# Neighbourhood attention: key planes loaded in pieces over several ticks, memory scores held eight ticks apart

## The chip, the cores and the metric

The kernel runs on one core of one Trainium2 chip. The metric is device time in microseconds (us) of one execution. Three runs of the kernel before give a median of 2871.68 us, with 2870.42 and 2873.8 as the lowest and the highest.

## What is computed

The layer mixes 2048 tokens of 1024 channels (a grid of 32 rows by 64 columns) in three ways in parallel, merges the three branches by gates, adds the result to the input, and ends with an MLP. Two of the branches matter here: attention over a window of 8 rows by 16 columns around each token (8 heads of 32 channels), and attention into 256 memory tokens (4 heads of 64 channels).

```python
def hybrid_layer(...):
    h = rmsnorm(x, g_mix)
    z = h @ w_in
    qk_m, v_m, o_m, i_pre, f_pre, qkv_na, q_mem, gate_pre = jnp.split(z, split_idx, axis=-1)
    ...                                     # mLSTM branch -> h_m
    q_na = rmsnorm(q_na, g_na_q) * (NA_HEAD_DIM ** -0.5)
    k_na = rmsnorm(k_na, g_na_k)
    h_na = neighbourhood_attention(q_na, k_na, v_na, rpb)
    h_mem = memory_cross_attention(q_mem, rmsnorm(mem, g_mem), w_mem_kv, g_mem_q, g_mem_k)
    gates = jax.nn.sigmoid(gate_pre).reshape(bsz, s, N_BRANCH, D_MODEL)
    y = (gates[:, :, 0] * (h_m @ w_proj_mlstm) + gates[:, :, 1] * (h_na @ w_proj_na)
         + gates[:, :, 2] * (h_mem @ w_proj_mem))
    x = x + y @ w_out
    u = rmsnorm(x, g_ffn) @ w_up
    return x + jnp.square(jax.nn.relu(u)) @ w_down
```

All of it is float32.

## The kernel before, in words

**Products.** A float32 operand is split into a high plane and a low plane, and a product is three matmuls: high by high, high by low, low by high (`mm3`, lines 243 to 245). A weight unit of 512 KB is loaded into one of three raw buffers (`wr`, line 183), split by ScalarE (line 186) and VectorE (line 187) into one of five `ws` buffers, and then multiplied.

**Phases.** Phase 1 goes over four blocks of 512 tokens (`block_a`): query and key projections of the window attention, convolution channels, values, mLSTM values, gate channels (blocks 2 and 3 only), output gates. Phase 2 runs the mLSTM chunks beside the other gate channels, phase 3 the merge, the output projection and the MLP. The window attention and the memory attention belong to phase 1: the first score of the window attention stands at 109.7 us of the profile and the last at 891.9 us.

**Ticks.** Within the projections of phase 1, the program stops after every six matmuls or so (`tick`), and each stream may put some instructions of its own there: `unit_stream` for the preparation of queries and keys, another one for the memory attention (`mem_unit`), and `na_stream` for the window attention. TensorE's order is written out by hand in this way. The other engines and the DMA queue are ordered by a scheduler at build time, which goes by priorities. Nearly all DMAs are issued by SyncE (SP), in one in-order queue; a DMA that has to wait for a buffer holds up those behind it.

**Window attention.** Its work comes in groups `g` of four grid rows and head halves `hg` of four heads: 16 pairs of (g, hg). A pair has one tile of queries, `naq` (96 partitions), and one of keys, `nak` (96 partitions, 4 heads, up to 704 columns). The 96 partitions hold 32 channels three times, so that one matmul (line 1084) makes the three products at once: queries as high, high, low and keys as high, low, high. `na_load_qk` fills both tiles from the scratch tensors `s_qs` and `s_ks` with six DMAs, each on 32 partitions and all four heads, issued in the tick in which the unit is made. Each pair is used by two units (column halves) of four heads, and each head has one score matmul (`na_scores`), one bias tile `nab` (line 1075, four buffers), a fused add and maximum on VectorE (line 1088), an exponential on ScalarE (line 1090), transposes (line 1104) and values (line 1118). Heads come every four ticks in blocks 0 to 2 (`na_rate` 1) and every two ticks in block 3 (`na_rate` 2).

**Memory attention.** `mem_unit` makes one unit for each 128 tokens: normalise, transpose, then twelve score matmuls (line 1314) into two score banks, a maximum on VectorE, four exponentials (line 1321) on ScalarE, transposes (line 1334) whose results ScalarE copies out (line 1336), and values (line 1344). Two units are live at once and both move in ticks with `tk` 3, thus every four ticks; `mem_at` only keeps two units from scoring in the same tick. The scores of the window and of the memory attention, and their values, share three PSUM banks (`mx`).

**Other traffic of phase 1 on the same queue.** The results of a gate group are stored from one of two `ev` buffers (`s_g`), and sums of the down weights are made beside them: `xt` loads (line 440) and `s_t` stores.

Of the kernel before, what the change touches and what calls it, by code (L numbers as in the profile page):

```python
# [13 lines left out]
F32 = mybir.dt.float32  # L14
# [16 lines left out]
EV = {1: 2, 2: 2, 3: 8}  # L31
XT = 2
PREP_V = 2
RMS_0, MEM_LOAD = 2, 2
NA_LATER, NA_VALUES = 5, 3
NAB = 4
LATER_3 = 4
# [45 lines left out]
class Body:  # L83
    def __init__(self, tc, a):
        self.tc, self.nc, self.a = tc, tc.nc, a
        self.n = 0
        self.later, self.ahead = LATER, AHEAD
        self.streams, self.qkq, self.memq, self.aux_end = [], [], [], False
        self.na_ready, self.na_end, self.na_rate, self.tk = [], False, 1, 0
        self.na_v, self.na_vfree, self.scored = [], 2, False  # L90
        self.ticks, self.mem_at = 0, -1
        self.jobs, self.out, self.split = [], (), ()
        self.wplan, self.wready = self.plan(), []

# [879 lines left out]
    def na_stream(self):  # L974


        todo, fetched, prev, ready = [], [], [], []
        biases, freed = [], [0] * NAB
        cur = last = None
        late = False  # L980
        while True:
            while self.na_ready:
                g = self.na_ready.pop(0)
                todo += [(g, hg, half) for hg in range(2) for half in range(2)]
            if todo and not fetched and (cur is None or cur["h"] > 0):
                last = self.na_unit(*todo.pop(0), last, 4 if cur else 8)
                fetched.append(last)
                biases += [(last, h) for h in range(4)]
            if cur is None and not fetched and self.na_end and not prev and not ready:
                return  # L990
            if self.tk % 2:
                due = ready.pop(0)[1] if ready and ready[0][0] >= NA_VALUES and not self.scored else None
                if due and (self.na_rate == 2 or late):
                    self.na_values(due)
                    due, late = None, False
                late = bool(ready and ready[0][0] >= NA_VALUES)
                self.scored = False
                step = self.tk == 3 or self.na_rate == 2
                if step and prev and prev[0][0] >= NA_LATER:
                    u, h, sb = prev.pop(0)[1]  # L1000
                    self.na_transpose(u, h, sb)
                    if h == 3:
                        ready.append([0, u])
                if due:
                    self.na_values(due)
                if step:
                    if cur is None and fetched and fetched[0]["wait"] <= 0:
                        cur = fetched.pop(0)
                    if cur:
                        while len(cur["bias"]) <= cur["h"]:  # L1010
                            self.na_bias(*biases.pop(0))
                            freed.pop(0)
                        freed.append(3)
                        prev.append([0, self.na_scores(cur, cur["h"])])
                        cur["h"] += 1
                        if cur["h"] == 4:
                            cur = None
            for u in fetched:
                u["wait"] -= 1
            for x in prev + ready:  # L1020
                x[0] += 1

            freed = [max(n - 1, 0) for n in freed]
            if biases and freed and not freed[0]:
                self.na_bias(*biases.pop(0))
                freed.pop(0)
            yield

    def na_load_qk(self, g, hg, kr0, nr):
        nc = self.nc  # L1030
        q = self.p_a.tile([96, 4, 256], F32R, name=f"naq{g}_{hg}", tag="naq", bufs=2)
        k = self.p_a.tile([96, 4, 11 * 64], F32R, name=f"nak{g}_{hg}", tag="nak", bufs=2)
        qs = self.scr["qs"][:, g, hg].rearrange("(h d) l f t -> d h l (f t)", d=32)
        ks = self.scr["ks"][:, hg, :, kr0 * 64:(kr0 + nr) * 64].rearrange("(h d) l t -> d h l t", d=32)

        for i, (lq, lk) in enumerate(((0, 0), (0, 1), (1, 0))):
            ds = slice(32 * i, 32 * i + 32)
            nc.sync.dma_start(q[ds].bitcast(F32), qs[:, :, lq])
            nc.sync.dma_start(k[ds, :, :nr * 64].bitcast(F32), ks[:, :, lk])
        return q, k  # L1040

    def na_unit(self, g, hg, half, before, wait):

        nc = self.nc
        kr0 = min(max(4 * g - 4, 0), 24)
        nr = 8 if g in (0, 7) else 11
        u = dict(g=g, hg=hg, half=half, nk=nr * 40, pts=[], h=0, wait=wait)
        u["qk"] = before["qk"] if half else self.na_load_qk(g, hg, kr0, nr)
        u["kts"] = [(3 * i, min(3, nr - 3 * i)) for i in range((nr + 2) // 3)]
        u["ho"] = before["ho"] if half else self.t("nho", [128, 2, 256], 1, F32R)  # L1050
        u["bias"] = []
        self.na_v.append(u)
        self.na_load_v()
        return u
# [242 lines left out]
    def mem_unit(self, b, t, z):  # L1297
        nc = self.nc
        yield from self.mem_norm(z)
        yield  # L1300
        q = self.t("mq", [128, 2, 2, 128], 2, F32R)
        self.mem_trans(z, q, self.gmqk[:, 0:1])
        yield

        while self.mem_at == self.ticks:
            yield
        es = []
        self.scored, self.mem_at = True, self.ticks
        psc = [self.ps("mx", (128, 2, 256)) for _ in range(2)]
        for p in range(2):  # L1310
            for i, (lq, lk) in enumerate(((0, 0), (0, 1), (1, 0))):
                for j in range(2):
                    js = slice(j * 64, j * 64 + 64)
                    nc.tensor.matmul(psc[j][:, p], q[js, lq, p], self.mk[js, lk, p], start=i == 0, stop=i == 2)
        nms, sms = ([self.small(2, "m") for _ in range(2)] for _ in range(2))
        for nm, pj in zip(nms, psc):
            nc.vector.tensor_reduce(nm, pj, AX.X, ALU.max, negate=True)
        for nm, sm, pj in zip(nms, sms, psc):
            e = self.t("me", [128, 2, 256], 4)
            for p in range(2):  # L1320
                nc.scalar.activation(e[:, p], pj[:, p], AF.Exp, bias=nm[:, p:p + 1], accum_out=sm[:, p:p + 1])
            es.append(e)
        for e, sm in zip(es, sms):
            rs = self.small(2, "m")
            nc.vector.reciprocal(rs, sm)
            nc.vector.tensor_tensor(e, e, rs.unsqueeze(2).to_broadcast([128, 2, 256]), ALU.mult)
        yield
        yield
        ptp = []
        for e in es:  # L1330
            tp = self.ps("tr", (128, 4, 128))
            for p in range(2):
                for kt in range(2):
                    nc.tensor.transpose(tp[:, 2 * p + kt], e[:, p, kt * 128:(kt + 1) * 128], self.ident)  # L1334
            pT = self.t("mpT", [128, 4, 128], 4)
            nc.scalar.activation(pT, tp, AF.Copy)
            ptp.append(pT)
            yield
        po = self.ps("mx", (128, 4, 128))
        for p in range(2):  # L1340
            for kt in range(2):
                for j in range(2):
                    h = 2 * p + j
                    nc.tensor.matmul(po[j * 64:(j + 1) * 64, p], self.mv[:, kt, h * 64:(h + 1) * 64], ptp[j][:, 2 * p + kt],  # L1344
                                     start=kt == 0, stop=kt == 1, tile_position=(0, j * 64))
        ho = self.t("mho", [128, 2, 2, 128], 1, F32R)
        nc.scalar.activation(ho[:, 0], po[:, 0:2], AF.Copy)
        nc.vector.tensor_tensor(ho[:, 1], po[:, 0:2], ho[:, 0].bitcast(F32), ALU.subtract)
        t0 = b * TB + t * 128
        self.store(self.scr["hmem"][:, :, :, t0:t0 + 128], ho.bitcast(F32))  # L1350
# [377 lines left out]
```

## Time and profile before

| | |
|---|---|
| median of the runs | 2871.68 us |
| the profiled execution, its own time | 2871.6 us |
| its span, from the first to the last instruction | 2869.9 us |
| TensorE busy | 2844.7 us |
| DMA, share of the 16 engines' span on the main queue | 67.1% |
| key loads (`nak`) | 36 of 352 KB and 12 of 256 KB |
| query loads (`naq`) | 48 of 128 KB |

In the lines of the trace, L12 is line 12 of the kernel. PE is TensorE (PEld its weight loads), DVE VectorE, ACT ScalarE, POOL GpSimd, SP SyncE. "Idle before" is the time that an engine waited ahead of an instruction, with the releaser that came last. "DMA share" is the mean busy share of the 16 DMA engines, GB/s what they moved. A line of the chain of waits has its start, its length and what it is.

### The profile page before, as it was taken

To read this page: it belongs to the slowest core of one execution; us is meant where nothing else is said; L and a number is where in the kernel's file an instruction comes from. 1 tells how busy PE (TensorE), PEld (TensorE's weight loads), DVE (VectorE), ACT (ScalarE), POOL (GpSimd) and SP (SyncE) were. 2 spreads that over 40 slices of the span, in tenths; PEclk is the share of its full clock that TensorE was granted. 3 is DMA by queue.
4 is the path that set the end of the run, shared out by engine and by line. 5 is a ranking of instruction groups with operands and counts; after the bars stand their busy time and mean duration, and the time that the engine had idled before them with its cause. 6 is when DMAs were issued, how large, how long until landed. Compare 5 with 4: busy or idle time off the path is not lost.

```text
span 2869.9 us, 41422 instructions
## 1 busy us (share of the span) xinstructions
PE 2844.7 (99%) x14920; PEld 2356.6 (82%) x14920; DVE 2050.7 (71%) x3516; ACT 1167.3 (41%) x2186; POOL 202.8 (7%) x254
## 2 busy tenths in 40 slices
PE   9999999999999999999999999999999999999999
PEld 8878888878887888888888888888788888888887
DVE  7676765577665556757699888866786998887666
ACT  6555654355543433532243334433312433343332
POOL 3221220011000122310000000000000000000000
PEclk9999999999999999999999999999999999999999
DMA  8776778876899888988444447756773444476553
GB/s 295 248 245 222 216 237 270 274 237 201 283 315 304 269 269 260 302 266 276 128 154 140 161 149 243 250 191 228 256 222 120 158 141 157 160 247 231 195 189 135
DMA packets 347053, 634.33 MB, mean 221 GB/s; under 512 B 29696, under 2 KB 152512, under 8 KB 346848
## 3 DMA queue, kind: packets, MB, share of 16 engines
q1 hardware_dynamic: 346432, 631.41, 67.1%
q8 instruction: 118, 1.93, 0.3%
q14 instruction: 87, 0.71, 0.1%
q10 hardware_dynamic: 416, 0.27, 0.0%
HBM read 454.68 MB, written 176.88 MB: 220 GB/s over the span
## 4 chain that ended last, share of the span: by engine, by line
PE 91%; DMA 4%; DVE 3%; issue 1%; ACT 1%; SPq 0%; POOL 0%; DVEq 0%; ACTq 0%; POOLq 0%
PE mm L243 28%; PE mm L245 27%; PE mm L244 27%; PE tr L1104 2%; PE mx L1118 1%; PE pn L873 1%; DMA wr<-in_w_units_dram 1%; PE mx L1084 1%; PE pn L876 1%; DVE ws L187 1%; PE mx L882 1%; PE mx L1344 0%; DMA nab<-in_rpb_dram 0%; PE tr L1334 0%; ACT ws L186 0%
## 5 line engine op out<-in xcount | busy, mean ns | idle before, releaser
L243 PE MATMUL mm<-X,ws 128*128 128x512 f32 x896 | 349.4, 390 | 0.0
L244 PE MATMUL mm<-X,ws 128*128 128x512 f32 x896 | 348.6, 389 | 0.0
L245 PE MATMUL mm<-X,ws 128*128 128x512 f32 x896 | 348.6, 389 | 0.0
L243 PE MATMUL mm<-hT,ws 128*128 128x512 f32 (+1 forms) x776 | 305.5, 394 | 0.7 <-ACT ev L544 0.7
L245 PE MATMUL mm<-hT,ws 128*128 128x512 f32 (+1 forms) x776 | 302.3, 390 | 0.0
L244 PE MATMUL mm<-hT,ws 128*128 128x512 f32 (+1 forms) x776 | 302.0, 389 | 0.0
L187 DVE TENSOR_TENSOR ws<-wr,ws 128x1024 fp32r<-128x1024 f32 (+2 forms) x195 | 239.5, 1234 | 70.1 <-ACT ws L186 68.7
L186 ACT ACTIVATE ws<-wr 128x1024 fp32r<-128x1024 f32 (+2 forms) x195 | 204.5, 1055 | 196.1 <-PE mm L245 134.2
L245 PE MATMUL mm<-X 128*128 128x512 f32 x616 | 239.7, 389 | 0.5 <-DVE X L1602 0.5
L243 PE MATMUL mm<-X 128*128 128x512 f32 x616 | 239.7, 389 | 0.1
L244 PE MATMUL mm<-X 128*128 128x512 f32 x616 | 239.6, 389 | 0.0
L213 ACT ACTIVATE ws<-wr 128x512 fp32r<-128x512 f32 x224 | 134.1, 628 | 233.1 <-PE mm L245 146.5
L243 PE MATMUL mm<-ws,hT 128*128 128x512 f32 (+2 forms) x624 | 220.1, 353 | 7.2 <-ACT ws L186 4.7
L244 PE MATMUL mm<-ws,hT 128*128 128x512 f32 (+2 forms) x624 | 216.9, 348 | 0.8 <-DVE ws L187 0.8
L245 PE MATMUL mm<-ws,hT 128*128 128x512 f32 (+2 forms) x624 | 217.1, 348 | 0.0
L1601 ACT ACTIVATE X<-X 128x1024 fp32r<-128x1024 f32 x109 | 115.6, 1062 | 215.5 <-DMA X<-s_s 107.1
L244 PEld LDWEIGHTS mm<-X,ws 128*128 128x128 f32 x896 | 168.2, 188 | 35.5 <-issue 0.5
L243 PEld LDWEIGHTS mm<-X,ws 128*128 128x128 f32 x896 | 168.2, 188 | 35.3 <-issue 0.5
L245 PEld LDWEIGHTS mm<-X,ws 128*128 128x128 f32 x896 | 168.2, 188 | 34.8
L1602 DVE TENSOR_TENSOR X<-X 128x1024 fp32r<-128x1024 f32 x109 | 132.6, 1223 | 62.1 <-ACT X L1601 61.3
L1618 DVE TENSOR_TENSOR acc<-acc,mm 128x512 f32<-128x512 f32 x192 | 126.2, 684 | 64.0 <-PE mm L245 63.9
L243 PEld LDWEIGHTS mm<-hT,ws 128*128 128x128 f32 x776 | 146.8, 189 | 30.4 <-issue 2.8
(296 smaller groups left out, 5974.1 us busy)
## 6 DMA issues: line engine op xcount, KB each, us to landing
wr<-in_w_units_dram SPq DMA_DIRECT2D x289, 512.0 KB
s_s<-u SPq DMA_DIRECT2D x32, 1024.0 KB
s_g<-ev SPq DMA_DIRECT2D x96, 256.0 KB
ev<-s_g SPq DMA_DIRECT2D x96, 256.0 KB
s_a<-u SPq DMA_DIRECT2D x96, 256.0 KB
X<-s_s SPq DMA_DIRECT2D x45, 512.0 KB
nab<-in_rpb_dram SPq DMA_DIRECT2D x96, 220.0 KB
xt<-in_w_units_dram SPq DMA_DIRECT2D x32, 512.0 KB
```

The lines of the kernel that those rows point to most:

```text
L186: s = nc.scalar.activation(w[:, 0, ks], raw[:, ks], AF.Copy)
L187: v = nc.vector.tensor_tensor(w[:, 1, ks], raw[:, ks], w[:, 0, ks].bitcast(F32), ALU.subtract)
L213: nc.scalar.activation(hi, src, AF.Copy)
L243: mm(out, lhs[0], rhs[0], start=first, stop=False)
L244: mm(out, lhs[0], rhs[1], start=False, stop=False)
L245: mm(out, lhs[1], rhs[0], start=False, stop=last)
L873: mm(pn[h % 2][:, h // 2], pt[:, h], v1[:, h], start=h < 2, stop=first)
L876: mm(pn[h % 2][:, h // 2], qw[hp, h // 2], C[hp, h // 2], start=False, stop=True)
L1104: nc.tensor.transpose(ptp[0:120, j], sb[:, j * 120:(j + 1) * 120], self.ident)
L1601: nc.scalar.activation(hi, src, AF.Copy)
L1602: nc.vector.tensor_tensor(lo, src, hi.bitcast(F32), ALU.subtract)
L1618: nc.vector.tensor_tensor(c, first[t] if first else c, p, ALU.add)
```

## The change

Three things are done. The loads of a pair's tiles are no longer issued on the spot: `na_load_qk` puts them into a list `na_loads`, and `na_stream` issues two of them in a tick (four in block 3), and all that are left when the unit becomes current. The keys' planes are laid out as high, high, low and the queries' as high, low, high. The keys' high plane is loaded head by head: one DMA writes 64 partitions from a source that has the 32 channels twice, by a leading step of length 2 and stride 0; the low plane comes in two DMAs of two heads. So a pair has nine DMAs in place of six, with the same number of bytes written. And a memory unit's scores wait until at least eight ticks have passed since another unit's.

```diff
-RMS_0, MEM_LOAD = 2, 2
+RMS_0, MEM_LOAD, MEM_STEP = 2, 2, 8
...
-        self.ticks, self.mem_at = 0, -1
+        self.ticks, self.mem_at, self.na_loads = 0, -99, []
...
                 return
+            self.na_load(2 * self.na_rate)
             if self.tk % 2:
...
                         cur = fetched.pop(0)
+                        self.na_load(9)
...
-        for i, (lq, lk) in enumerate(((0, 0), (0, 1), (1, 0))):
-            ds = slice(32 * i, 32 * i + 32)
-            nc.sync.dma_start(q[ds].bitcast(F32), qs[:, :, lq])
-            nc.sync.dma_start(k[ds, :, :nr * 64].bitcast(F32), ks[:, :, lk])
+        both = lambda h: ks[:, h, 0].unsqueeze(0).to_broadcast([2, 32, nr * 64])
+        for i, l in enumerate((0, 1, 0)):
+            self.na_loads.append((q[32 * i:32 * i + 32].bitcast(F32), qs[:, :, l]))
+        for h in range(0, 4, 2):
+            for j in (h, h + 1):
+                self.na_loads.append((k[0:64, j, :nr * 64].bitcast(F32), both(j)))
+            self.na_loads.append((k[64:96, h:h + 2, :nr * 64].bitcast(F32), ks[:, h:h + 2, 1]))
         return q, k
+
+    def na_load(self, n):
+
+        for _ in range(min(n, len(self.na_loads))):
+            self.nc.sync.dma_start(*self.na_loads.pop(0))
...
-        while self.mem_at == self.ticks:
+        while self.ticks - self.mem_at < MEM_STEP:
             yield
```

Two places of the instruction order, which stand word for word as the built program has them. The first is SyncE's queue where the pair (6, 1) is loaded, before; `wr` is a weight unit, `nab` a bias tile, `s_hmem` a store.

```order
L1075 DMA nab_0_1_3_9094<-in_rpb_dram 128x440
L1038 DMA naq_1_9102<-s_qs 32x4x256
L1039 DMA nak_1_9103<-s_ks 32x4x704
L1038 DMA naq_1_9102<-s_qs 32x4x256
L1039 DMA nak_1_9103<-s_ks 32x4x704
L1038 DMA naq_1_9102<-s_qs 32x4x256
L1039 DMA nak_1_9103<-s_ks 32x4x704
L183 DMA wr_9037<-in_w_units_dram 128x1024
L105 DMA s_hmem<-mho_9126 512x1x128
L1075 DMA nab_1_0_0_9146<-in_rpb_dram 128x440
```

The same place after the change; `nav` loads are values of the window attention, `s_hna` stores its output.

```order
L1085 DMA nab_0_1_3_9126<-in_rpb_dram 128x440
L1050 DMA nak_1_9135<-s_ks 64x1x704
L183 DMA wr_9069<-in_w_units_dram 128x1024
L1078 DMA nav_0_1_9104<-s_vna 120x3x128
L1079 DMA nav_0_1_9104<-s_vna 80x128
L105 DMA s_hna<-nho_8274 256x1x256
L1050 DMA nak_1_9135<-s_ks 64x1x704
L1050 DMA nak_1_9135<-s_ks 32x2x704
L1050 DMA nak_1_9135<-s_ks 64x1x704 x2
L1085 DMA nab_1_0_0_9174<-in_rpb_dram 128x440
```

The three queries have moved ahead of this place, the first piece of the keys stands ahead of the weight unit, and three of the remaining pieces of 64 partitions and one of 32 stand ahead of the bias tile of the next unit. The last one of 32 follows behind that.

The second place is ScalarE around the values of the unit (1, 0, 0), whose copy is line 1124 of before and 1134 of after. `me` are the memory scores' exponentials. Before:

```order
L1107 ACTIVATE npt_3593<-tr_3588 120x512
L1321 ACTIVATE me_3576,sm_3572<-mx_3556,sm_3570 128x256 x2
L1321 ACTIVATE me_3579,sm_3573<-mx_3557,sm_3571 128x256 x2
L1090 ACTIVATE nsb_344,sm_3599<-nsb_344,sm_3597 128x440
L1124 ACTIVATE nho_2884<-mx_3626 128x4x32
```

And after:

```order
L1117 ACTIVATE npt_3573<-tr_3568 120x512
L479 ACTIVATE zna_3606<-mm_3530 128x512
L936 ACTIVATE sq_3621<-zna_3606 128x512
L1134 ACTIVATE nho_2884<-mx_3575 128x4x32
L1100 ACTIVATE nsb_344,sm_3601<-nsb_344,sm_3599 128x440
L420 ACTIVATE xt_3950,sm_3852<-xt_3950 128x1024
```

The second memory unit's exponentials no longer stand between the transposed scores and the values there; they come later, behind two squares of `x` tiles (line 420).

## Prediction

> **What bounds the kernel now.** I read the page first, then the chain of waits in order of time, what TensorE waited for, and last the DMA traffic, stretch by stretch, between one load of keys and the next. Shares of the page and TensorE's own waits:
>
> ```profile
> PE 2844.7 (99%) x14920; PEld 2356.6 (82%) x14920; DVE 2050.7 (71%) x3516; ACT 1167.3 (41%) x2186; POOL 202.8 (7%) x254
> PE mm L243 <- ACT ws L186: 4.7, 1, 4.7
> PE mx L1084 <- issue: 2.4, 1, 2.4
> PE tr L1104 <- ACT mpT L1336: 2.1, 1, 2.1
> PE mx L1118 <- ACT me L1321: 1.3, 1, 1.3
> ```
>
> TensorE is busy for 2844.7 of 2869.9 us, and the change leaves its instructions as they are in number and kind. So it can take away no more than a few waits of TensorE, and the four above, 10.5 us together, are those near the code that it touches. What it can add has no such limit. The rows of the chain of waits (start, length, what) that are no TensorE work tell where phase 1 hangs on transfers:
>
> ```profile
> 263.84 5.71 DMA wr<-in_w_units_dram
> 274.62 4.81 DMA xt<-in_xT_dram
> 566.36 5.91 DMA nab<-in_rpb_dram
> 572.29 9.64 DMA wr<-in_w_units_dram
> 827.18 6.05 DMA nak<-s_ks
> 833.29 8.18 DMA nab<-in_rpb_dram
> 858.97 6.45 DMA naq<-s_qs
> ```
>
> Near 270, 570 and from 827 on, a transfer that lands later is time lost; elsewhere it has a lead. At the last load the lead is gone (issue on SP, then the score that uses the load, and the next wait for a bias):
>
> ```profile
> 859.32 0.43 SPq L1039 DMA_DIRECT2D nak<-s_ks  x1
> 866.85 0.60 PE L1084 MATMUL mx<-nak,naq 96*128 96x320 f32 x1 [2.37 <-issue]
> 868.17 0.49 DVE L1088 CUSTOM_DVE_ANT_0 nsb<-mx,nab 128x320 f32<-128x320 f32 x1 [2.98 <-DMA nab<-in_rpb_dram]
> ```
>
> The last piece of keys is issued 7.5 us ahead of its score, and TensorE waits 2.37 us there; right after that VectorE waits 2.98 us for a bias that was queued behind. How much room the DMA engines have is read from their share in the stretches that begin with a load of keys (length, then share and GB/s at the row's end):
>
> ```profile
> core 0: us, PE busy (x) PEld busy (x) DVE busy (x) ACT busy (x) POOL busy (x), PEclk, DMA share, GB/s
> 277.00:312.00 35.00, 32.70 (x206) 26.47 (x203) 27.51 (x68) 19.51 (x47) 4.55 (x4) 1.00 0.76 217
> 435.00:508.00 73.00, 73.00 (x470) 59.70 (x469) 43.41 (x90) 33.88 (x74) 0.00 (x0) 1.00 0.80 265
> 508.00:568.00 60.00, 60.00 (x341) 49.69 (x340) 30.52 (x62) 22.60 (x42) 0.00 (x0) 1.00 0.83 267
> 568.00:600.00 32.00, 26.64 (x137) 20.96 (x136) 18.51 (x48) 11.85 (x23) 0.00 (x0) 0.89 0.88 267
> 600.00:644.00 44.00, 44.00 (x273) 36.29 (x272) 34.14 (x84) 26.17 (x52) 8.43 (x6) 1.00 0.76 225
> 760.00:793.00 33.00, 33.00 (x245) 27.07 (x244) 22.77 (x58) 17.99 (x43) 0.00 (x0) 1.00 0.89 277
> 793.00:824.00 31.00, 31.00 (x220) 25.27 (x219) 19.89 (x49) 14.83 (x32) 0.00 (x0) 1.00 1.05 321
> 824.00:854.00 30.00, 30.00 (x206) 24.59 (x205) 19.51 (x55) 14.74 (x33) 0.00 (x0) 1.00 1.00 321
> 854.00:905.00 51.00, 48.63 (x290) 39.21 (x289) 32.53 (x85) 22.18 (x47) 0.00 (x0) 0.97 0.92 297
> 905.00:960.00 55.00, 54.25 (x285) 45.07 (x285) 23.34 (x36) 19.78 (x29) 2.53 (x9) 1.00 0.90 300
> ```
>
> In block 3, from 793 to 854 us, the sixteen engines have no room at all by this account.
>
> **The change part by part. The price of a piece.** Two rows for 555 to 580 us in 40 slices of 0.625 us give the rates, the first in tenths of busy share, the second in GB/s:
>
> ```profile
> DMA  9758203995799999999989998999999999999989
> GB/s 407 282 196 260 55 20 131 347 172 125 256 393 400 413 403 410 413 406 302 138 301 400 406 344 309 397 417 266 213 187 198 208 169 245 222 238 194 175 129 263
> ```
>
> With all engines busy, weights and stores on 128 partitions move at 400 to 417 GB/s, some 25.5 GB/s an engine. From the slice at 572.5 us on, when queries and keys on 32 partitions are under way, nine slices with the engines as busy average 208 GB/s. So the shape of a transfer already decides here how much of the sixteen engines is used.
>
> The new loads of the high plane write 64 rows of 704 numbers, 180,224 bytes, from a source whose first step has two entries. No transfer of before has such a source, so its price has two ends. Dealt over all engines at 208 GB/s, a piece takes 0.9 us of them. Cut only along the first step, into two parts, it lies on two engines, 90,112 bytes each, and takes 3.5 us of those two, which all other transfers need as well. I take the second end: a step of two gives no sixteen equal parts, and in the rows above the loads whose first step is 32 are already the slower ones than those with 128.
>
> [...]
>
> **The net load of two engines.** A pair with 704 columns has four such pieces: 14.2 us of the two engines. The low plane, 360,448 bytes on 32 partitions, takes 1.7 us of all at 208 GB/s; the three key loads that go, 1,081,344 bytes, took 5.2 us. Net: 14.2 + 1.7 - 5.2 = 10.7 us more. With 512 columns (the first two and the last two pairs) it is 10.3 + 1.3 - 3.8 = 7.8 us.
>
> **Where it fits.** Room is length times (1 - share). In 277 to 312 it is 8.4 us, so 2.3 us don't fit; 508 to 568: 10.2, 0.5 over; 568 to 600: 3.8, 6.9 over; 600 to 644: 10.6, 0.1 over. The remaining ones ahead of 760 have more than they need (435 to 508: 14.6 us). From 760 the four stretches have 3.6, 0, 0 and 4.1 us, so that 7.1, 10.7, 7.8 and 3.7 us don't fit. Together that is 9.8 us early and 29.3 us late.
>
> **What of it TensorE feels.** A weight unit, a bias or a store that is spread over sixteen engines has landed only when its part on the two crowded ones has, so the backlog is met by everything that is issued behind it. Early, the 2.3 and the 6.9 us fall where the chain already runs through `wr`, `xt` and `nab`: 9.2 us. The 0.6 us are covered. Late, there is some lead at first. The pair of 793 us:
>
> ```profile
> 793.45 0.42 SPq L1039 DMA_DIRECT2D nak<-s_ks  x1
> 796.03 0.30 SPq L1039 DMA_DIRECT2D nak<-s_ks  x1
> 806.73 0.45 PE L1084 MATMUL mx<-nak,naq 96*128 96x440 f32 x1
> ```
>
> From the last issue to the score are 10.7 us; the 6.05 us of `nak` in the chain leave 4.7 us. That is used up once, since the next loads come on top of a backlog. At the end, 905 to 960 has 5.5 us of room, which takes that much of the backlog after the last key is in. Late: 29.3 - 4.7 - 5.5 = 19.1 us. The slower matmuls that follow a long wait (0.60 us for the score at 866.85) aren't added: the two engines catch up meanwhile.
>
> **The spreading.** The DMAs grow by three a pair, 48 issues of the 0.4 us seen in the rows above on a queue that waits for buffers most of the time: nothing, while SP is ahead. As the two orders show, the pieces let one weight unit pass in the middle but still put most of a pair's bytes ahead of the next bias tile. That heads 2 and 3 come later than heads 0 and 1 helps a load by one or two heads, but the bias behind it gets no such respite, and with none of the lead left at 868 us I count nothing.
>
> **The memory scores.** Eight ticks in place of four take the second unit's exponentials out of the way of the window attention's values. The wait of 1.3 us for `me` goes; what is late next there is the copy of the transposed scores ahead of it, which had been done. The one of 2.1 us for `mpT` I count half, because a square of an `x` tile that waits for a DMA stands on ScalarE before it:
>
> ```profile
> 176.92 4.50 DMA xt<-in_x_dram
> 181.51 1.15 ACT xt L420 x2
> 184.14 1.44 PE mx L1118 x24
> ```
>
> That wait can also grow, and the second order shows two more of these squares ahead of the exponentials. The cost of spacing is bounded by minus 3.4 us (both waits) and plus 4.5 us (another transfer met by ScalarE); I take minus 2.3. The waits of 4.7 and 2.4 us for transfers stay, since these land no sooner.
>
> **The sum** is made against the profiled execution, 2871.6 us, which stands within 0.1 us of the median: 9.2 + 19.1 - 2.3 = +26.0 us, 2897.6 us. A measurement of this kernel tells about 0.2% from no change, 5.7 us.
>
> **The rivals.** What TensorE loses behind the last load of keys, beside the wait itself, is seen in four of the matmuls after it (start, length):
>
> ```profile
> 867.25 0.63 PE L243 MATMUL mm<-hT,ws 128*128 128x512 f32 x1
> 867.68 0.63 PE L244 MATMUL mm<-hT,ws 128*128 128x512 f32 x1
> 870.60 0.39 PE L243 MATMUL mm<-hT,ws 128*128 128x512 f32 x1
> 870.82 0.39 PE L244 MATMUL mm<-hT,ws 128*128 128x512 f32 x1
> ```
>
> *All sixteen engines carry the pieces* (faster, 0.12). It decides by a piece's price at the end of 0.9 us: then a pair costs the engines 3.6 + 1.7 us against 5.2, the same, and only the earlier start and the order by heads are left. The score at 866.85 no longer waits (2.4 us, and 1.4 us of slow matmuls behind it: from 866.85 to 869.9 some seven start 0.43 us apart, as the first two rows do, and not 0.22 as the last two), the memory scores give 2.3, and half of the 4.7 us for weights at 578 goes as keys and weights alternate: -8.5 us, 2863. For it speaks that somebody may split the repeated source further on its way to the engines; against it, that the program as built hands it on with the step of two.
>
> [...]
>
> *Two engines, but hidden* (no change, 0.10). Counted by bytes, 760 to 905 has more room: 277, 321, 321 and 297 GB/s over their lengths are 43.9 MB, at 408 GB/s 107.5 of the 145 us, and the 5.3 MB on 32 partitions of these four pairs at 208 GB/s cost 12.5 us more. Then 25 us are free against 37 us of net load, and of the 12 that don't fit the leads of 4.7 and 5.5 us take all but 1.8: 2871.6 - 2.3 + 1.8 = 2871. Against it speaks that both the score and the bias of the last pair wait already.
>
> *The backlog feeds on itself* (much slower, 0.14). Gate groups leave through two `ev` buffers, and the weights through three raw ones. If each of the twelve loads that I count as fitting in the gaps cost a wait of 2 to 3 us on top of the sum, since a burst of 14 us falls into the few us of one load, that is 30 us: 2928.
>
> **How the numbers follow.** The forecast has 0.64, the rivals 0.12, 0.10 and 0.14. The forecast's own range goes from 2880 (10 us of late overflow less, half of the early waits covered) to 2915 (no lead at all, 10.2 us, and the scores' plus 4.5 in place of minus 2.3). Up to 2864 below and 2922 above, two in ten are left out: about half of the first rival and most of the last. Faster by over 0.2% is most of the first rival, 0.10; within it 0.12, the hidden case and the first one's rest; slower 0.78.
>
> **What would show it.** Right: DMA share in 760 to 905 falls below that of before, while waits for `nab`, `wr` and `nak` grow in TensorE's, VectorE's and ScalarE's lists; the time is lost between 760 and 930 us, some near 570, none after phase 1; a piece of 180 KB takes as long to land as a weight unit of 512 KB, 5 us or more. The score that waited for `me` follows its neighbour at once. Wrong: the slices with keys under way stay at 200 GB/s with all engines busy, and the last pair's score has no wait. Then the pieces are dealt out over sixteen, and the price, the first step of the sum, has failed.

## The result, and the profile after

The changed kernel takes 2959.71 us (median of 4 runs, 2954.76 to 2964.37) against 2872.18 us before (4 runs): 87.5 us more, ratio 1.0302, 95% interval 1.0289 to 1.0314. The forecast was slower by 26 us, with a range up to 2922 us. Cause and sign were as forecast, the size was not, and this part is mainly about where the other 61.5 us came from. The profiled execution of after took 2961.6 us, span 2959.9, so 90.0 us more than the profiled one of before. TensorE's part of it, from the page:

```profile
PE 2865.5 (97%) x14920; PEld 2371.1 (80%) x14920; DVE 2046.7 (69%) x3516; ACT 1158.6 (39%) x2186; POOL 200.8 (7%) x254
```

**All of it is lost in phase 1.** Busy time by stretch, first before, then after (length, PE, PEld, DVE, ACT and POOL busy with their counts, granted clock, DMA share, GB/s). The second row of each is what follows phase 1, 1909 us long in both:

```profile
0.00:960.00 960.00, 942.02 (x5954) 785.72 (x5955) 633.05 (x1413) 498.67 (x1036) 126.48 (x132) 0.99 0.81 258
960.00:2869.00 1909.00, 1902.69 (x8967) 1570.83 (x8965) 1417.62 (x2103) 668.68 (x1151) 76.30 (x122) 1.00 0.61 202
```

```profile
0.00:1050.00 1050.00, 962.86 (x5956) 800.59 (x5957) 629.83 (x1414) 490.36 (x1036) 123.86 (x132) 0.96 0.74 236
1050.00:2959.00 1909.00, 1902.66 (x8966) 1570.48 (x8964) 1416.84 (x2103) 668.28 (x1150) 76.89 (x122) 1.00 0.61 202
```

From 960 us of before and 1050 us of after the two are alike. Ahead of that TensorE is idle for 87.1 us where it was idle for 18.0, 69.2 us more; and for the same matmuls it is busy 20.8 us longer, at a granted clock of 0.96 instead of 0.99. Idle time and slower matmuls together are the 90.0 us.

**Where in phase 1.** The same score matmuls in both kernels, before and then after (start, length):

```profile
256.34 0.44 PE L1084 MATMUL mx<-nak,naq 96*128 96x440 f32 x1
345.62 0.45 PE L1084 MATMUL mx<-nak,naq 96*128 96x440 f32 x1
602.03 0.44 PE L1084 MATMUL mx<-nak,naq 96*128 96x440 f32 x1
757.52 0.45 PE L1084 MATMUL mx<-nak,naq 96*128 96x440 f32 x1
882.18 0.39 PE L1084 MATMUL mx<-nak,naq 96*128 96x320 f32 x1
```

```profile
259.74 0.47 PE L1094 MATMUL mx<-nak,naq 96*128 96x440 f32 x1
367.62 0.45 PE L1094 MATMUL mx<-nak,naq 96*128 96x440 f32 x1
633.56 0.44 PE L1094 MATMUL mx<-nak,naq 96*128 96x440 f32 x1
820.48 0.45 PE L1094 MATMUL mx<-nak,naq 96*128 96x440 f32 x1
969.67 0.39 PE L1094 MATMUL mx<-nak,naq 96*128 96x320 f32 x1
```

The lag goes from 3.4 to 22.0, 31.5, 63.0 and 87.5 us. So 24.5 us are lost between 757 and 882 us of before's time (and 2.5 more up to the end of phase 1), where the forecast had 19.1, and 63.0 ahead of that, where it had 9.2.

**What waits.** Waits of the whole phase, before and then after (who for what, us in total, times, longest):

```profile
ACT ws L186 <- DMA wr<-in_w_units_dram: 39.7, 28, 4.2
DVE xt L392 <- DMA xt<-in_xT_dram: 9.7, 6, 3.4
DVE xt L567 <- DMA xt<-in_w_units_dram: 4.5, 3, 3.3
```

```profile
PE tr L1114 <- DVE sm L1102: 11.5, 1, 11.5
PE mx L1128 <- ACT me L1331: 9.1, 3, 7.1
...
PE mx L1094 <- DMA xt<-in_w_units_dram: 7.8, 1, 7.8
...
PE mx L1094 <- DMA nak<-s_ks: 4.7, 1, 4.7
...
ACT ws L186 <- DMA wr<-in_w_units_dram: 82.9, 31, 8.8
ACT ev L591 <- DMA s_g<-ev: 46.8, 9, 9.8
DVE xt L392 <- DMA xt<-in_xT_dram: 43.0, 9, 16.1
DVE xt L567 <- DMA xt<-in_w_units_dram: 42.3, 8, 12.9
```

One wait of TensorE, 4.7 us, is put down to the keys. The one of 7.8 us, put down to an `xt` unit, stands ahead of the first score of a pair, at 916.17 us, whose pieces had been issued from 903.81 us on. A score reads no `xt` unit, so this wait is probably for the keys too. Together that is 12.5 us. What else has grown are waits for weights, inputs and gate groups, which the change does not touch, and TensorE stands behind the engines that wait for those. One such place, in full. The DMA engines from 764 to 784 us of after, in 40 slices of 0.5 us (tenths of the sixteen engines' time, then GB/s):

```profile
DMA  1499479999999631111111111111100000948996
GB/s 45 187 371 154 131 233 376 341 199 199 189 188 289 152 76 42 54 34 51 51 56 51 49 55 49 53 51 52 46 34 25 0 0 0 131 139 319 369 287 246
```

From 771.5 to 778.5 us the slices move some 50 GB/s (34 to 56) at a tenth of the sixteen engines' time. At the 25.5 GB/s an engine that the prediction read from the rows of before, that is two engines, and fourteen with nothing to do. The four pieces of a pair had been issued between 753 and 761 us, and an `xt` unit at 764.34. From the chain of waits, from VectorE's timeline, and from TensorE's (start, length, in brackets the wait ahead):

```profile
764.34 13.95 DMA xt<-in_w_units_dram
```

```profile
764.72 0.69 DVE L1336 TENSOR_TENSOR me<-me,sm 128x512 f32<-128x512 f32 x1
778.31 0.69 DVE L567 TENSOR_TENSOR xt<-xt,xt 128x512 f32<-128x512 f32 x1 [12.90 <-DMA xt<-in_w_units_dram]
...
781.26 0.14 DVE L1102 RECIPROCAL sm<-sm 128x1 f32<-128x1 f32 x1
```

```profile
784.17 1.08 PE L1114 MATMUL tr<-ident,nsb 128*120 128x128 f32 x4 [11.52 <-DVE sm L1102]
...
785.42 0.63 PE L243 MATMUL mm<-hT,ws 128*128 128x512 f32 x1
785.84 0.63 PE L244 MATMUL mm<-hT,ws 128*128 128x512 f32 x1
...
788.28 0.39 PE L244 MATMUL mm<-hT,ws 128*128 128x512 f32 x1
788.51 0.40 PE L245 MATMUL mm<-hT,ws 128*128 128x512 f32 x1
```

The unit of 512 KB needs 13.95 us, where the four `xt` loads in before's chain of waits in phase 1, of the same size, took 4.50 to 5.57 us. It lands at 778.29 us, just as the plateau of the two engines ends, which fits that its part on these two waited for the pieces. VectorE waits 12.90 us for it with the window softmax queued behind, TensorE 11.52 us for that softmax, and then its matmuls start 0.43 us apart for 3 us until they are back at 0.23. The granted clock is 0.50 from 785 to 788 us and 0.98 from 788 to 791 us.

The place is no exception. In slices of 0.5 us from 100 us to the end of phase 1, those at a tenth of the engines' time and 45 to 57 GB/s are 195 in after, with up to eleven in a row, and 9 in before, with no two in a row.

The share of the DMA engines in two stretches of the late part, as the prediction had it to fall (before had 0.89 to 1.05 from 760 to 905 us):

```profile
750.00:800.00 50.00, 38.48 (x199) 31.64 (x198) 25.65 (x57) 23.52 (x54) 2.63 (x3) 0.90 0.68 219
850.00:900.00 50.00, 50.00 (x354) 40.82 (x353) 28.90 (x69) 20.80 (x46) 0.00 (x0) 1.00 0.72 234
```

The chain of waits of after has five key loads in phase 1, of 6.7 to 14.0 us from issue to landing, as the prediction expected of its pieces (5 us or more).

### The profile page after: what moved, and what is told of

Same layout as the page of the kernel before. It is cut to its first block, busy times and chain, and to the rows that moved or that the text cites. A ratio compares the mean times of both kernels' runs of the same rounds, so it can differ in the third digit from the quotient of the medians.

```text
span 2959.9 us, 41518 instructions
## 1 busy us (share of the span) xinstructions
PE 2865.5 (97%) x14920; PEld 2371.1 (80%) x14920; DVE 2046.7 (69%) x3516; ACT 1158.6 (39%) x2186; POOL 200.8 (7%) x254
## 4 chain that ended last, share of the span: by engine, by line
PE 72%; DMA 15%; DVE 7%; issue 2%; ACT 2%; SPq 1%; POOL 0%; DVEq 0%; ACTq 0%; POOLq 0%
PE mm L243 23%; PE mm L245 22%; PE mm L244 22%; DMA xt<-in_w_units_dram 3%; DMA wr<-in_w_units_dram 2%; DMA nak<-s_ks 2%; DMA nav<-s_vna 2%; DMA s_t<-xt 1%; DMA xt<-in_xT_dram 1%; DVE ws L187 1%; PE pn L873 1%; DMA xt<-in_x_dram 1%; ACT ws L186 1%; PE tr L1114 1%; DVE cy L678 1%
## 5 line engine op out<-in xcount | busy, mean ns | idle before, releaser
L244 PE MATMUL mm<-ws,hT 128*128 128x512 f32 (+2 forms) x624 | 219.3, 351 | 8.9 <-DVE ws L187 8.9
L243 PE MATMUL mm<-ws,hT 128*128 128x512 f32 (+2 forms) x624 | 222.5, 357 | 5.0 <-ACT ev L499 2.7
L245 PE MATMUL mm<-ws,hT 128*128 128x512 f32 (+2 forms) x624 | 219.3, 351 | 0.0
L243 PEld LDWEIGHTS mm<-hT,ws 128*128 128x128 f32 x776 | 148.6, 191 | 33.0 <-issue 5.9
L245 PEld LDWEIGHTS mm<-hT,ws 128*128 128x128 f32 x776 | 147.7, 190 | 31.7
```

What stands on the lines that cost most here:

```text
L243: mm(out, lhs[0], rhs[0], start=first, stop=False)
L244: mm(out, lhs[0], rhs[1], start=False, stop=False)
L245: mm(out, lhs[1], rhs[0], start=False, stop=last)
```

## The experiments

Times are medians. A difference is taken to the kernel before on the same chip, whose median was 2871.2 to 2873.6 us. All runs are of the whole kernel, and where an edit changes the order of rows, queries and keys change alike.

### The pieces on sixteen engines

```diff
 for j in (h, h + 1):
-    self.na_loads.append((k[0:64, j, :nr * 64].bitcast(F32), both(j)))
+    for i in (0, 1):
+        self.na_loads.append((k[32 * i:32 * i + 32, j, :nr * 64].bitcast(F32), ks[:, j, 0]))
```

> The changed kernel, but each piece of the high plane is two loads of 32 rows instead of one of 64 rows from a repeated source; bytes, spreading over ticks, order of heads and spacing of the memory scores stay, and SP issues 64 loads more. Theory (the repeated source puts a piece on two engines): nearly all of the 87.5 us goes, 2862 to 2880 us, and the median landing of a piece falls below 6 us. Rival (the pieces come too late because they are issued one by one over the ticks): it stays slow, 2930 us or more.

2873.19 us, ratio 1.0002 (0.9992 to 1.0012). The whole 87.5 us is gone with nothing changed but the shape of the high plane's loads. The rival of late, single issues is out. How long a piece takes to land is not on record for this run; no key load stands in its chain of waits.

### The repeated source alone

```diff
-for i, (lq, lk) in enumerate(((0, 0), (0, 1), (1, 0))):
+both = lambda h: ks[:, h, 0].unsqueeze(0).to_broadcast([2, 32, nr * 64])
+for i, (lq, lk) in enumerate(((0, 0), (1, 0), (0, 1))):
     ds = slice(32 * i, 32 * i + 32)
     nc.sync.dma_start(q[ds].bitcast(F32), qs[:, :, lq])
-    nc.sync.dma_start(k[ds, :, :nr * 64].bitcast(F32), ks[:, :, lk])
+    if i == 0:
+        for h in range(4):
+            nc.sync.dma_start(k[0:64, h, :nr * 64].bitcast(F32), both(h))
+    if i == 2:
+        nc.sync.dma_start(k[ds, :, :nr * 64].bitcast(F32), ks[:, :, lk])
```

> The kernel before, but its two loads of the high plane are replaced by four loads of 64 rows from a repeated source, issued at once where those stood; no spreading, and the memory scores as before. Theory (two engines): it alone costs most of the change, 2930 to 3000 us. Rival (the spreading costs): within 10 us of the kernel before.

2964.25 us, ratio 1.0319 (1.0305 to 1.0333): the loss, without spreading and without spacing.

### The spacing alone

```diff
-RMS_0, MEM_LOAD = 2, 2
+RMS_0, MEM_LOAD, MEM_STEP = 2, 2, 8
...
-while self.mem_at == self.ticks:
+while self.ticks - self.mem_at < MEM_STEP:
```

> The kernel before with the memory scores eight ticks apart and nothing else. The prediction's term: 2.3 us less, 2869 to 2870 us. Rival: the spacing delays values or makes ScalarE meet transfers, 4.5 us more or beyond.

2866.32 us, ratio 0.9982 (0.9973 to 0.9991), so 5 us faster, from 2.6 to 7.8. The sign is that of the forecast's term of 2.3 us, the size at or above it. In the list of TensorE's waits of this run the rows of before for `me` (1.3 and 1.0 us) and for `mpT` (2.1 us) are gone.

### Half of the heads

```diff
+if j % 2:
+    for i in (0, 1):
+        self.na_loads.append((k[32 * i:32 * i + 32, j, :nr * 64].bitcast(F32), ks[:, j, 0]))
+else:
     self.na_loads.append((k[0:64, j, :nr * 64].bitcast(F32), both(j)))
```

> The changed kernel, but only heads 0 and 2 load their high plane from the repeated source; heads 1 and 3 take two loads of 32 rows each. The load on the two engines falls by about half, some 100 us over phase 1. Theory as a matter of room (two engines are over-full in the changed kernel, and are not with half): 0 to 25 us over the kernel before. Rival (each piece on two engines is late by itself, so the loss goes by their number): about 44 us over it, 35 to 50.

2888.60 us, ratio 1.0057 (1.0043 to 1.0070), 15.7 us more. Half of the load brings a fifth of the loss: it does not go by the number of pieces.

### The copy inside

```diff
-both = lambda h: ks[:, h, 0].unsqueeze(0).to_broadcast([2, 32, nr * 64])
+both = lambda h: ks[:, h, 0].unsqueeze(1).to_broadcast([32, 2, nr * 64])
-for i, l in enumerate((0, 1, 0)):
-    self.na_loads.append((q[32 * i:32 * i + 32].bitcast(F32), qs[:, :, l]))
+for h in range(4):
+    self.na_loads.append((q[0:64, h].bitcast(F32), qs[:, h]))
+self.na_loads.append((q[64:96].bitcast(F32), qs[:, :, 0]))
```

> The changed kernel with the two steps of the repeated source exchanged: 32 rows outside, the copy of stride zero inside, so that a piece is still one load of 64 rows that reads each row twice; queries load to match (rows of their two planes alternate), in five loads for three. Theory (the count of the outermost step decides, and 32 gives all sixteen engines): as with two loads of 32 rows, 2862 to 2885 us. Rival (a source that is read twice, or 64 rows by one load, is slow by itself): 2930 us or more.

2853.03 us, ratio 0.9934 (0.9919 to 0.9949): 20.6 us faster than before, and 107 us faster than the change with its two steps in the other order. So it is not reading rows twice that costs, but the order of the two steps. Phase 1 of this kernel and the rest:

```profile
0.00:942.00 942.00, 936.25 (x5960) 783.88 (x5961) 630.47 (x1414) 495.83 (x1036) 130.91 (x132) 1.00 0.82 264
942.00:2851.00 1909.00, 1901.84 (x8962) 1570.44 (x8960) 1416.61 (x2103) 667.77 (x1150) 74.32 (x122) 1.00 0.61 202
```

TensorE is idle for 5.8 us of phase 1 where it was for 18.0, and its matmuls take 5.8 us less: all 18 us by which this phase is shorter.

### An outermost step of two without repetition

```diff
-for i, l in enumerate((0, 1, 0)):
-    self.na_loads.append((q[32 * i:32 * i + 32].bitcast(F32), qs[:, :, l]))
+for i, l in enumerate((0, 0, 1, 1)):
+    self.na_loads.append((q[16 * i:16 * i + 16].bitcast(F32), qs[i % 2::2, :, l]))
+self.na_loads.append((q[64:96].bitcast(F32), qs[:, :, 0]))
-    self.na_loads.append((k[0:64, j, :nr * 64].bitcast(F32), both(j)))
+    for i in (0, 1):
+        self.na_loads.append((k[32 * i:32 * i + 32, j, :nr * 64].bitcast(F32),
+                              ks[:, j, 0].rearrange("(e o) t -> o e t", o=2)))
```

> Two loads of 32 rows for each head's high plane, nothing repeated, but the 32 rows in the order even, odd, so that the source's outermost step has two entries with a stride that isn't zero; queries load to match, in five loads for three. Theory (the outermost count): as slow as the changed kernel, 2930 to 2980 us. Rival (the stride of zero is what costs): 2862 to 2885 us.

2939.67 us, ratio 1.0243 (1.0221 to 1.0265), 66 us more. It is slow without any stride of zero. The load that it puts on two engines is that of the change, and the loss 66 us and not 87.5: the load alone does not fix the size, and why this run lost less is not settled. Its DMA rows from 530 to 550 us, again in slices of 0.5 us, show the same plateau at two engines:

```profile
DMA  6821999993111111159996899999999521294189
GB/s 223 316 98 73 378 399 411 407 407 137 52 49 49 53 53 49 55 217 346 370 241 172 344 401 377 369 399 231 261 190 307 130 83 77 87 317 117 45 208 251
```

Seven slices in a row, from 535 to 538.5 us, move 49 to 55 GB/s at a tenth of the engines' time. At 25.5 GB/s an engine that is two engines, for a step of two, as in after.

### Transfers that nothing reads

Both kernels are the one before, with four more transfers for each pair into a tensor in DRAM that is never read. They differ in the order of two steps:

```diff
+dm=d("s_dm", [16, 4, 64, 704]),
...
+for h in range(4):
+    nc.sync.dma_start(self.scr["dm"][2 * g + hg, h, :, :nr * 64],
+                      ks[:, h, 0].unsqueeze(0).to_broadcast([2, 32, nr * 64]))   # the second: unsqueeze(1), [32, 2, ...]
```

> The kernel before with its own loads, and for each pair four more transfers of the high plane, 64 rows from a source with the copy outermost, into a tensor in DRAM that nothing reads. Theory (two crowded engines delay whatever is spread over all sixteen): slow though no key comes later on its own account, 2930 to 3010 us. Rival (only the keys' own lateness costs): below 2890 us.

> As the run before, with the copy inside: the same bytes and the same number of transfers, dealt over sixteen engines. Both theories: 10.75 MB more, 27 us of all engines at 400 GB/s, most of it hidden, 2868 to 2895 us. If it is as slow as its twin, the bytes or the issues cost and not the two engines.

2983.50 us, ratio 1.0386 (1.0367 to 1.0405), against 2896.41 us, ratio 1.0086 (1.0070 to 1.0102). The same bytes cost 23 us with the copy inside and 110 with it outside: 87 us for the order of the two steps alone, as in the change, though here every key that is read comes by the loads of before. With the copy outside the plateau of two engines is there again: from 680 to 688.5 us seventeen slices of 0.5 us in a row are at a tenth, with 45 to 56 GB/s. As in after, the waits for weights grow with the copy outside (39.7 us in before), here together with those for biases (5.0 us in before); with the copy inside those for weights do not. First the run with the copy outside, then the one with it inside:

```profile
ACT ws L186 <- DMA wr<-in_w_units_dram: 111.7, 42, 18.6
DVE nsb L1091 <- DMA nab<-in_rpb_dram: 42.3, 11, 9.5
```

```profile
ACT ws L186 <- DMA wr<-in_w_units_dram: 39.5, 24, 6.7
```

### Source, spacing and spreading apart

The first is the kernel before with the copy inside, its loads issued at once; the second adds the spacing; the third keeps the six loads of before, and spreads and spaces them.

```diff
+both = lambda h: ks[:, h, 0].unsqueeze(1).to_broadcast([32, 2, nr * 64])
+for h in range(4):
+    nc.sync.dma_start(q[0:64, h].bitcast(F32), qs[:, h])
+    nc.sync.dma_start(k[0:64, h, :nr * 64].bitcast(F32), both(h))
+nc.sync.dma_start(q[64:96].bitcast(F32), qs[:, :, 0])
+nc.sync.dma_start(k[64:96, :, :nr * 64].bitcast(F32), ks[:, :, 1])
```

> The kernel before, its loads issued all at once where they stood and its memory scores as they were; only the high plane comes as four loads of 64 rows with the copy inside, and the queries of the first 64 rows as four loads to match. If the gain of 20 us with the copy inside and all the rest of the change came from the shape of these loads: 2850 to 2862 us. If it came from the spreading and the spacing: 2866 to 2876 us.

> The run before with the memory scores eight ticks apart. If the spreading over ticks is worth nothing, this equals the changed kernel with the copy inside, 2851 to 2856 us; if it is worth something, the difference is its price.

The third, with `na_load` as in the change:

```diff
 for i, (lq, lk) in enumerate(((0, 0), (0, 1), (1, 0))):
     ds = slice(32 * i, 32 * i + 32)
-    nc.sync.dma_start(q[ds].bitcast(F32), qs[:, :, lq])
-    nc.sync.dma_start(k[ds, :, :nr * 64].bitcast(F32), ks[:, :, lk])
+    self.na_loads.append((q[ds].bitcast(F32), qs[:, :, lq]))
+    self.na_loads.append((k[ds, :, :nr * 64].bitcast(F32), ks[:, :, lk]))
```

> The spreading without the new loads: the six loads of the kernel before, taken from a queue two at a tick, with the memory scores eight ticks apart. The prediction counted the spreading as nothing: then it equals the spacing alone, 2864 to 2869 us. Rival (later keys and biases cost): 2870 us or more. Rival (keys and weights alternate, which helps): below 2862 us.

Ratios 0.9956 (0.9943 to 0.9968), 0.9946 (0.9934 to 0.9959) and 1.0017 (1.0008 to 1.0027); 2859.63, 2856.86 and 2876.24 us. With the copy inside, the loads give 11.6 us by themselves; spacing and spreading add some 3 us each, little enough for the intervals to overlap. With the six loads of before, spreading takes back what the spacing gave: 1.0017 beside 0.9982 are 10 us. That is against the forecast, which counted it as nothing.

### Four engines, and a control

```diff
+for i in range(8):
+    self.na_loads.append((q[8 * i:8 * i + 8].bitcast(F32), qs[i % 4::4, :, i // 4]))
+self.na_loads.append((q[64:96].bitcast(F32), qs[:, :, 0]))
...
+    self.na_loads.append((k[32 * i:32 * i + 32, j, :nr * 64].bitcast(F32),
+                          ks[:, j, 0].rearrange("(e o) t -> o e t", o=4)))
```

> As the run with an outermost step of two and nothing repeated, but the 32 rows in four groups, so that the outermost step has four entries; queries load to match in groups of eight rows. Theory (a piece lies on as many engines as the outermost step has entries): four engines get some 105 us each in phase 1, as two do when only half of the heads are repeated, so about the same loss, 2880 to 2905 us. Rival (any split outermost step is slow, whatever its count): 2925 us or more; or only a step of two is: 2862 to 2880 us.

2920.55 us, ratio 1.0172 (1.0154 to 1.0189), 49 us more: between the two expectations. The control has the same nineteen loads for a pair, with rows in their plain order and keys as two loads of 32 rows:

> The run with four groups, with its nineteen loads for a pair and its queries in groups of eight rows, but the keys in two loads of 32 rows whose outermost step is 32. If four crowded engines made the 49 us of that run: 2870 to 2885 us here. If the many small loads, or keys that come later because they queue behind them, made them: 2905 us or more.

2900.05 us, ratio 1.0091 (1.0073 to 1.0109). So 26 us of the 49 come with the nineteen loads, the queries in groups of eight rows among them, and some 23 are left for the outermost step of four. That is near the 15.7 us of half the heads on two, which would put as much on each crowded engine. That four engines carry these pieces is shown less directly than the two: slices of 0.5 us at two tenths and 92 to 110 GB/s are 36 in this run and 9 in the control, seldom several in a row.

### One and three heads

The edit is that of half the heads, with `if j == 3:` (three heads repeat) and `if j:` (one head repeats) in place of `if j % 2:`.

> As the run with half of the heads, but heads 0, 1 and 2 repeat and head 3 takes two loads of 32 rows: some 165 us more for two engines in phase 1. If the loss begins where those engines fill (two heads 16 us, four 88): well under three quarters of 88, 2900 to 2930 us. If it goes by the number of late pieces: 66 us, 2935 us or more.

> Head 0 alone repeats: some 55 us more for the two engines. Room theory: within 6 us of the run with two loads of 32 rows for every head, 2867 to 2879 us. By the number of late pieces: 22 us more, 2890 us or more.

2903.28 us, ratio 1.0106 (1.0084 to 1.0128), and 2887.10 us, ratio 1.0047 (1.0029 to 1.0065). With none, one, two, three and four heads repeated the loss is 0, 13.5, 15.7, 29.7 and 87.5 us. Neither theory has this curve: the first head costs far more than room alone says, the fourth costs 58 us, about as much as the other three twice over. The slices at the plateau of two engines grow from run to run, with one, two, three and four heads 47, 71, 124 and 195 (11 with the copy inside). Phase 1 of one, two and three heads:

```profile
0.00:976.00 976.00, 946.67 (x5956) 790.02 (x5957) 632.36 (x1414) 494.04 (x1036) 124.68 (x132) 0.99 0.80 254
```

```profile
0.00:979.00 979.00, 948.69 (x5958) 791.37 (x5959) 630.87 (x1414) 494.32 (x1036) 127.50 (x132) 0.99 0.80 254
```

```profile
0.00:990.00 990.00, 950.95 (x5960) 791.77 (x5961) 627.92 (x1414) 490.84 (x1036) 131.10 (x132) 0.99 0.79 251
```

An estimate of the work of a crowded engine: length times DMA share is the mean over sixteen (781, 783, 782 us, and 777 with four heads). The pieces of a head that is repeated in all pairs, 12 of 3.53 us and 4 of 2.57 at 25.5 GB/s, are 52.7 us on each of two engines and an eighth of that in the mean. So the two have 781 + 46 = 827, 783 + 92 = 875, 782 + 138 = 920 and 777 + 184 = 961 us to do. Phase 1 of before lasts 960 us: with three heads there is a little time left, with four there is none.

## Why the prediction was right in cause and sign, and wrong in size

**The price of a piece**, two engines: right, by the plateau at two engines and by the runs that change the order of steps alone.

**The net load of two engines** was too small, 160 us where the estimate above gives some 184 (961.4 less the 777.6 of before, 960 at 0.81; the shares are rounded, so each of these may be 5 us off). The pieces were sized as they are (211 us), but the loads that go were credited with 3.5 us a pair more than the low plane (2.5 with 512 columns), 52 us in all. The mean of the other work fell from 778 us to 751 (777 less the pieces' 26), by 27, half of that credit.

**Where it fits** is the step that failed. The prediction said of the stretches ahead of 760 us, but for four, that they "have more than they need", and let only 39 of the 160 us count. By the estimate the room of the whole phase was 182 us (960 less 778) and the need 184, so that nothing was left over wherever it lay. And room in a stretch is not enough. From 602 to 760 us before had

```profile
602.00:760.00 158.00, 158.00 (x1098) 133.75 (x1097) 117.00 (x260) 88.05 (x189) 26.29 (x24) 1.00 0.74 231
```

which is 41 us of room. The forecast had 0.1 us there that did not fit, and took it as covered; 31.5 us were lost. The unit of 764 us of after, which belongs there, came 12.9 us late with fourteen engines idle. It was wanted as soon as it was issued, and paid for the burst ahead of it; by the estimate the pieces of one pair are 14 us of two engines. The waits for `xt` on VectorE grew from 14.2 to 85.3 us (the rows of L392 and L567 together). The loss isn't even: between 367.62 and 633.56 us of after the lag grew by 9.5 us only.

That this was the step is seen with fewer heads as well. Worked out as in the prediction, with a quarter, half and three quarters of its net load against the same rooms and leads, 0, 2 and 14 us would be felt, and 28 with four heads. Measured were 13.5, 15.7, 29.7 and 87.5 us, and nothing with none. So the sum is some 14 to 16 us short while the two engines have time left, and 59 us short where they have none. Nor does it have the place. The scores of 709.92, 757.52 and 882.18 us of before are with three heads at

```profile
712.81 0.36 PE L1098 MATMUL mx<-nak,naq 96*128 96x440 f32 x1
767.99 0.71 PE L1098 MATMUL mx<-nak,naq 96*128 96x440 f32 x1
908.02 0.39 PE L1098 MATMUL mx<-nak,naq 96*128 96x320 f32 x1
```

which is 2.9 us lost up to the first, where the sum has 4.2, then 7.6 in a stretch that has room by the sum, and 15.4 late, where it has 9.7. What the first 14 us are made of is not settled.

**What of it TensorE feels.** Late, 24.5 us for 19.1. The slower matmuls were left out with the reason that the engines catch up meanwhile. They are 20.8 us, a quarter of the loss. That they were not covered because the two engines are hardly ever free, so that catching up was another use of the same missing room, fits the estimate but is not shown by itself. After the wait of 11.52 us matmuls start 0.43 us apart from 785.42 to 787.98, at the granted clock of 0.50.

**The spreading** was counted as nothing, and is 10 us with the loads of before, and nothing that can be told with the copy inside. **The memory scores**: 5 us for 2.3, by the spacing alone. In the changed kernel itself the gain can't be seen, and the wait for `me` is 9.1 us there and not gone, since ScalarE's exponentials now stand behind its waits for weights: at 840.12 us its split of a weight unit (line 186) had waited 8.34 us, and the exponentials that follow at 841.56 us end the longest of these waits.

**The rivals.** The backlog that feeds on itself, 2928 us with a chance of 0.14, named what happened, a burst that falls into the few us of one load; at 2 to 3 us for each load it was still 32 us short. For all sixteen engines the prediction had 2863 us. With the two plain loads it is 2873, where the spreading costs what the spacing gives, and with the copy inside, which keeps the load of 64 rows, 2853. Hidden behind the room that is left by bytes: it fails by the same sum as the forecast, since it gave the two engines 25 us of room late and let the early loads go free. Two figures of the prediction come out otherwise from its own terms: the lower end of its range, 2880, as 2883, and four pieces, 14.2 us, as 14.1; nothing hangs on either.

## What to carry to other kernels

Look at the outermost step of a transfer's source: with two entries it lay on two engines here (slices at a tenth, some 50 GB/s), with or without a repetition, and an `xt` unit of 512 KB behind such pieces took 13.95 us to land. Put a copy inside, not outside: the kernel took 2853.03 us with it inside and 2959.71 us with it outside. To price such a load, sum the whole work of the crowded engines over the phase and hold it against its length. Here the loss was steep once that was full (29.7 us with three heads, 87.5 with four), but 13.5 us were lost with one head already, with room left. Then add the slower matmuls behind every long wait, 20.8 us here.

## What the runs showed that was not expected

- The kernel with the copy inside beats both: 2853.03 us, 0.66% under before (0.51 to 0.81%). Why one load of 64 rows that reads each row twice beats two loads of 32 rows, by 20 us with spreading and spacing, isn't settled: there are 32 issues less in phase 1, the queries come by head, and the two rows of a copy lie side by side.
- Bytes that nothing reads cost 23 us with the copy inside, for 10.75 MB, 27 us of all engines if they move at 400 GB/s. By that estimate little of them was hidden, at a mean share of 0.81; whether the bytes cost this or the 64 issues was not tried.
- Nineteen loads for a pair, with queries in groups of eight rows, cost 27 us more than thirteen. Whether the number or the small groups do it wasn't tried.
